# A one-core hybrid transformer layer on Trainium2: normalising products pinned behind the second slot's logits, two gate projections moved forward

## The chip, the cores and the metric

The kernel runs on one core of one Trainium2 chip. The metric is the device time of one execution in microseconds (us). The median of three runs of the kernel before is 888.42 us (888.24 to 889.56).

The engines have short names in what follows: PE multiplies matrices, DVE, ACT and POOL work on vectors, SP issues the DMA transfers. Every engine works through its own queue in order.

## The reference

One layer of a decoder (512 tokens, width 1024, fp32) with three mixers side by side:

```python
h = rms_norm(x, g_mix)
qa, ka, va, xb, gb, qc, kc, vc, gates = split(h @ w_in)
o_a = sum(softmax(lses, axis=0) * outs)       # outs, lses of the 3 groups of mixer A
o_b = rg_lru_branch(xb, gb)
o_c = moba_attention(qc, kc, vc)
gt = sigmoid(gates).reshape(B, S, 3, D)
merged = gt[:, :, 0] * (o_a @ p_a) + gt[:, :, 1] * (o_b @ p_b) + gt[:, :, 2] * (o_c @ p_c)
x = x + merged @ w_out
gate, up = split(rms_norm(x, g_ffn) @ w_gu)
x = x + (silu(gate) * up) @ w_down
return rms_norm(x, g_final)
```

Mixer A is a dilated window attention in 3 groups of 4 heads (dilations 1, 4, 16); slot j of the three groups is combined by their softmax denominators. Mixer B is a convolution and an RG-LRU scan times a GeLU gate, mixer C a block-sparse attention with 8 heads.

## The kernel before

**Products.** Every fp32 number is held as a high and a low part (hi, lo), and every product is three matmuls (`mm3`, lines 200 to 202): hi by hi, lo by hi, hi by lo. A projection (`project`) of 128 output columns is 8 such triples, 24 matmuls of 128x512, into one of the 8 PSUM banks.

**Weights.** `chunk_plan` lists the 512 KB chunks of weights in the order in which PE will want them. Each chunk passes through three engines: SP loads it (wraw, three buffers), ACT casts the high part (whi, L178, four buffers), and POOL, for chunks 7 to 61, subtracts the low part (wlo, L183, four pieces of 128x256); DVE does that for the others.

**x and its normalised form.** X holds the eight pairs (hi, lo) of x times the norm's gain g. The norm's factor per token, rb, is known only later, so projections that use X are multiplied by rb (or rq, for queries) when they leave PSUM (L479). XN holds the pairs of x·g·rb and needs no such step. `reload` fetches x again (8 DMAs) and `renorm` makes XN: for each of 8 tiles one product on DVE (L926, x·g·rb), then `split`: a cast on ACT for hi (L249) and a subtraction on DVE for lo (L250). Projections of half 1 of mixer A, of mixer C, of mixer B and all 24 gates use XN.

**Mixer A in slots.** The heads are worked on in four slots j = 0 to 3, each with its own dictionary d0 to d3. `la(j)` gives the steps for the logits, which are woven between the matmuls of another projection: group 0 with 128x256 logits and their row minima (L562), then the two class groups, whose bias is added at L579 and whose minima (m, stp) are taken at L585. `wa(d)` takes the exponentials on ACT (L594), adds two sums on DVE (L710) and sends the slot's statistics through DRAM (exch) and back in another order. `wa2(d)` works out each group's weight (ee on ACT, the rest on DVE) and scales the probabilities P (L599). `ta(d)` turns P on PE (L608, L622), and ACT and DVE split the result into ph, pl (L611, L612) and pp (L628, L629). `xa(d)` multiplies with the values (L659, L780).

**Gates.** `gate` is one projection and a tanh; the results wait as z tiles until `merge` uses them. Of 24, the table `EARLY` says how many are worked out at which place ahead of merge; merge does the others, staying `G_LEAD` = 2 ahead. The place names are a2, a3, v0 and so on; a new place has to stand in `EARLY`, in `chunk_plan` and in the program.

**What sets the order.** A scheduler reorders each engine's instructions by its own model of their times, within what the data allow; `keep_in_program_order` pins an instruction to its place in the program. The program's own order around the change is: values of A with slot 0's logits woven in, `wa(d0)`, `fa(0, 2, 0)` and `fa(0, 2, 1)` (the q and k projections of the last pair of half 0), `wa2(d0)`, `renorm`, slot 1's logits in the first values of C, `wa(d1)`, `ta(d0)` in the second values of C, `fa(1, 0, 0)`, `xa(d0)`, `fa(1, 0, 1)`.

Of the kernel before, what the change touches and what calls it, by code (L numbers as in the profile page):

```python
# [9 lines left out]
AF = mybir.ActivationFunctionType  # L10
ALU = mybir.AluOpType
# [7 lines left out]
KT = 8  # L19
# [24 lines left out]
N_POOL = 62  # L44
AHEAD = 2

EARLY = {"a2": 1, "a3": 1, "v0": 2, "v1": 2, "v2": 1, "c0": 1, "c1": 1, "l1": 1, "l2": 1, "l3": 1, "l4": 1,
         "b0": 1, "b1": 4}
G_LEAD = 2
N_WARM = 10  # L50
# [5 lines left out]
def chunk_plan():  # L56
# [3 lines left out]
    def a(h, i, w):  # L60
        plan.append(("ma", (OFF_QA, OFF_KA)[w], A_PAIRS[h][i]))

    def v(off, g):
        plan.extend(("v", off + g * 256, kh) for kh in range(2))
# [18 lines left out]
    plan.extend(("vv", OFF_VA + 256, kq) for kq in range(4))  # L83
    a(0, 2, 0)
    a(0, 2, 1)
    v(OFF_VC, 0)
    v(OFF_VC, 1)
    for n in range(2):
        a(1, n, 0)
        a(1, n, 1)  # L90
    a(1, 2, 0)
    g("a2")
    a(1, 2, 1)
# [38 lines left out]
def layer_kernel(tc, x0p, xT, wts, tab, oneh, msk, idn, gfin, out):  # L132
    nc = tc.nc
# [3 lines left out]
    with (  # L137
# [91 lines left out]
        def project(act, kind="m", steps=(), first=0):  # L229
            return weave(project_g(act, kind), 8, steps, first)  # L230
# [39 lines left out]
        X = []  # L270
# [403 lines left out]
                qk[pair[n] + (w,)] = t[n]  # L674

        def fa(half, i, w, steps=(), first=0):
            scaled = half == 1
            ea(project(XN if scaled else X, "ma", steps, first), half, i, w, scaled)

        def st_part(st, s, o):  # L680
# [225 lines left out]
        def gate(steps=()):  # L906
            ng[0] += 1
            z = slot(F32, "z")
            nc.scalar.activation(z, project(XN, "m", steps), AF.Tanh, scale=0.5)
            return z  # L910


        XN = []
# [6 lines left out]
                nc.sync.dma_start(xt, xT[k])  # L920
                x_again.append(xt)

        def renorm(ks):
            for k in ks:
                xt = x_again[k]
                nc.vector.scalar_tensor_tensor(xt, in0=xt, scalar=prm[:, k : k + 1], in1=rb,  # L926
                                               op0=ALU.mult, op1=ALU.mult)
                XN.append(split(xt))

        zs = []  # L930
# [2 lines left out]
        def early(place, steps=()):  # L933

            n = EARLY[place]
            for i in range(n):
                zs.append(gate(steps if i == n - 1 else ()))
# [25 lines left out]
        wa(d0)  # L963
        fa(0, 2, 0)
        fa(0, 2, 1)
        wa2(d0)
        renorm(range(8))
        d1, st = la(1)
        VC.append(values_out(values_mm(st, 12)))
        wa(d1)  # L970
        st = ta(d0)
        VC.append(values_out(values_mm(st)))
        fa(1, 0, 0)
# [2 lines left out]
        wa2(d1)  # L976
        fa(1, 1, 0)
        fa(1, 1, 1)
        st = ta(d1)
        fa(1, 2, 0, st)  # L980
        early("a2")
# [360 lines left out]
```

## Time and profile before

| | us |
|---|---|
| median of 3 runs | 888.42 |
| lowest, highest | 888.24, 889.56 |
| profiled execution | 888.6 |
| its span | 886.6 |
| PE busy in it | 875.2 (99%) |
| DVE, ACT, POOL busy | 472.8, 399.3, 283.9 |

The profile is of one execution. Its span runs from the first to the last instruction; 2.0 us of the 888.6 lie around it. The chain of work that ended last runs through PE for 88% of the span. PE's busy time counts a matmul as busy at whatever clock it was granted, so a slow clock shows in no idle time; the profile gives the granted clock by itself, as a share of 2.4 GHz, and its lower level, 1.2 GHz, reads 0.50.

### The profile page before, as it was taken

To read this page: it belongs to the slowest core of one execution; us is meant where nothing else is said; L and a number is where in the kernel's file an instruction comes from. 1 tells how busy PE (TensorE), PEld (TensorE's weight loads), DVE (VectorE), ACT (ScalarE), POOL (GpSimd) and SP (SyncE) were. 2 spreads that over 40 slices of the span, in tenths; PEclk is the share of its full clock that TensorE was granted. 3 is DMA by queue.
4 is the path that set the end of the run, shared out by engine and by line. 5 is a ranking of instruction groups with operands and counts; after the bars stand their busy time and mean duration, and the time that the engine had idled before them with its cause. 6 is when DMAs were issued, how large, how long until landed. Compare 5 with 4: busy or idle time off the path is not lost.

```text
span 886.6 us, 11269 instructions
## 1 busy us (share of the span) xinstructions
PE 875.2 (99%) x4166; PEld 737.4 (83%) x4166; DVE 472.8 (53%) x922; ACT 399.3 (45%) x692; POOL 283.9 (32%) x328
## 2 busy tenths in 40 slices
PE   9999999999999999999999999999999999999996
PEld 7897988888888888888888888888888888888885
DVE  7498947566665656647425445444444444322226
ACT  7376754664675567762323434333223332222213
POOL 2157364655543434675111312111222111000004
PEclk9999999999999999999999999999999999999999
DMA  7247332652322221232223322222222222222202
GB/s 276 93 158 111 94 127 88 108 133 96 95 95 84 84 95 47 97 119 95 95 95 119 119 92 84 88 94 95 95 95 99 100 103 104 96 95 95 95 24 96
DMA packets 40279, 90.28 MB, mean 102 GB/s; under 512 B 13988, under 2 KB 15780, under 8 KB 40224
## 3 DMA queue, kind: packets, MB, share of 16 engines
q1 hardware_dynamic: 34048, 88.26, 30.8%
q10 hardware_dynamic: 5824, 0.98, 0.7%
q8 instruction: 33, 0.54, 0.3%
q0 software_dynamic: 352, 0.33, 0.2%
q14 instruction: 22, 0.18, 0.1%
HBM read 87.34 MB, written 2.20 MB: 101 GB/s over the span
## 4 chain that ended last, share of the span: by engine, by line
PE 88%; DVE 4%; issue 3%; POOL 2%; DMA 2%; ACT 1%; DVEq 0%; POOLq 0%; ACTq 0%
PE ps L200 23%; PE ps L201 23%; PE ps L202 23%; PE ps L1189 12%; POOL wlo L183 2%; DMA wraw<-in_wts 2%; PE ps L659 2%; PE ps L608 1%; PE ps L555 1%; PE ps L554 1%; DVE y L1234 1%; DVE lo L250 0%; PE ps L622 0%; PE ps L780 0%; ACT junk L1220 0%
## 5 line engine op out<-in xcount | busy, mean ns | idle before, releaser
L178 ACT CAST whi<-wraw 128x1024 fp32r<-128x1024 f32 (+1 forms) x149 | 154.6, 1039 | 274.9 <-issue 101.5
L183 POOL TENSOR_TENSOR wlo<-wraw,whi 128x256 fp32r<-128x256 f32 x220 | 169.6, 803 | 181.1 <-ACT whi L178 181.0
L200 PE MATMUL ps<-hi,whi 128*128 128x512 f32 x520 | 205.2, 395 | 0.0
L201 PE MATMUL ps<-lo,whi 128*128 128x512 f32 x520 | 202.9, 390 | 0.0
L202 PE MATMUL ps<-hi,wlo 128*128 128x512 f32 x520 | 202.7, 390 | 0.0
L183 DVE TENSOR_TENSOR wlo<-wraw,whi 128x1024 fp32r<-128x1024 f32 (+1 forms) x94 | 117.5, 1250 | 115.5 <-ACT whi L178 115.5
L200 PE MATMUL ps<-uhi,whi 128*128 128x512 f32 x352 | 137.9, 392 | 0.0
L202 PE MATMUL ps<-uhi,wlo 128*128 128x512 f32 x352 | 137.1, 389 | 0.0
L201 PE MATMUL ps<-ulo,whi 128*128 128x512 f32 x352 | 136.9, 389 | 0.0
L202 PEld LDWEIGHTS ps<-hi,wlo 128*128 128x128 f32 x520 | 97.6, 188 | 20.6
L200 PEld LDWEIGHTS ps<-hi,whi 128*128 128x128 f32 x520 | 97.7, 188 | 18.8
L201 PEld LDWEIGHTS ps<-lo,whi 128*128 128x128 f32 x520 | 97.8, 188 | 18.5
L1163 POOL TENSOR_TENSOR av<-sg,uu 128x512 f32<-128x512 f32 x22 | 45.7, 2077 | 198.5 <-DVE sg L1161 198.5
L202 PEld LDWEIGHTS ps<-uhi,wlo 128*128 128x128 f32 x352 | 66.1, 188 | 14.0
L201 PEld LDWEIGHTS ps<-ulo,whi 128*128 128x128 f32 x352 | 66.1, 188 | 13.5
L200 PEld LDWEIGHTS ps<-uhi,whi 128*128 128x128 f32 x352 | 66.1, 188 | 13.3
L1189 PE MATMUL ps<-wlo,hi 128*128 128x512 f32 (+1 forms) x180 | 57.7, 384 | 0.0
L1189 PE MATMUL ps<-whi,lo 128*128 128x512 f32 (+1 forms) x180 | 57.7, 384 | 0.0
L1189 PE MATMUL ps<-whi,hi 128*128 128x512 f32 (+1 forms) x180 | 57.1, 384 | 0.0
L1159 DVE TENSOR_TENSOR uu<-ps,rb 128x512 f32<-128x512 f32 x22 | 15.2, 690 | 64.9 <-PE ps L202 64.9
L1222 POOL TENSOR_TENSOR y<-x,gf 128x512 f32<-128x512 f32 (+1 forms) x8 | 9.7, 1229 | 108.3 <-DVE x L1212 107.9
L200 PE MATMUL ps<-whi,xhi 128*128 128x256 f32 (+1 forms) x128 | 40.4, 318 | 0.3 <-DVE stn L562 0.3
(232 smaller groups left out, 1236.2 us busy)
## 6 DMA issues: line engine op xcount, KB each, us to landing
wraw<-in_wts SPq DMA_DIRECT2D x145, 512.0 KB, 3.2
xt<-in_xT SPq DMA_DIRECT2D x15, 256.0 KB, 5.5
bias<-relb SPq DMA_DIRECT2D x8, 256.0 KB, 6.9
xr<-in_xT SPq DMA_DIRECT2D x8, 256.0 KB, 2.7
out<-y SPq DMA_DIRECT2D x7, 256.0 KB, 2.4
wraw<-in_wts SPq DMA_DIRECT2D x4, 256.0 KB, 4.9
bias<-relb SPq DMA_DIRECT2D x4, 128.0 KB, 4.5
bias<-relb SPq DMA_DIRECT2D x8, 64.0 KB, 5.1
```

The source lines that it names most:

```text
L178: nc.scalar.copy(hi[:, cc], raw[:, cc])
L183: eng.tensor_sub(lo[:, dd], raw[:, dd], f32(hi[:, dd]))
L200: nc.tensor.matmul(o, lh, rh, start=start, stop=False)
L201: nc.tensor.matmul(o, lh, rl, start=False, stop=False)
L202: nc.tensor.matmul(o, ll, rh, start=False, stop=stop)
L554: nc.tensor.matmul(bk, qh[:, qc], kk[:, k0 : k0 + nn], start=True, stop=False)
L555: nc.tensor.matmul(bk, ql[:, qc], kk[:, k0 : k0 + nn], start=False, stop=True)
L659: nc.tensor.matmul(po[:, o0 : o0 + n], vf(kt), p, start=(i == 0), stop=(i == len(mms) - 1))
L1159: nc.vector.tensor_mul(uu, pu, r2)
L1163: nc.gpsimd.tensor_mul(av, sg, uu)
L1189: nc.tensor.matmul((acc[tb][hf] if o is None else o)[:, cc], l[:, t], r[:, hf * 512 + cc.start : hf * 512 + cc.stop], start=((k == 0 or fi ...
L1222: eng.tensor_mul(y2[hf][:, cc], x, gf[hf][:, cc])
```

## The change

Four things change. `EARLY` gains the places a0 and a1, one gate each. a0 stands behind `fa(0, 2, 1)`, ahead of slot 1's logits; a1 behind `fa(1, 1, 1)`, ahead of `ta(d1)`. Merge then has two gates fewer to do. `renorm` moves from ahead of `la(1)` to behind `wa(d1)`; all eight products come first, each pinned in program order, and the eight splits follow. Since XN does not exist yet at a0 and at `fa(1, 0, *)`, these use X: the gate gets a multiplication by rb on DVE ahead of its tanh, and q and k of `fa(1, 0, *)` the multiplication that half 0 has. In the changed kernel the lines of the code shown below are two to ten further down: 926 becomes 933, 562 becomes 564, 612 becomes 614.

```diff
-EARLY = {"a2": 1, "a3": 1, "v0": 2, "v1": 2, "v2": 1, "c0": 1, "c1": 1, "l1": 1, "l2": 1, "l3": 1, "l4": 1,
+EARLY = {"a0": 1, "a1": 1, "a2": 1, "a3": 1, "v0": 2, "v1": 2, "v2": 1, "c0": 1, "c1": 1, "l1": 1, "l2": 1, "l3": 1, "l4": 1,
         "b0": 1, "b1": 4}
...
     a(0, 2, 0)
     a(0, 2, 1)
+    g("a0")
     v(OFF_VC, 0)
     v(OFF_VC, 1)
     for n in range(2):
         a(1, n, 0)
         a(1, n, 1)
+    g("a1")
     a(1, 2, 0)
...
         def fa(half, i, w, steps=(), first=0):
-            scaled = half == 1
+            scaled = (half, i) > (1, 0)
...
             z = slot(F32, "z")
-            nc.scalar.activation(z, project(XN, "m", steps), AF.Tanh, scale=0.5)
+            if XN:
+                nc.scalar.activation(z, project(XN, "m", steps), AF.Tanh, scale=0.5)
+            else:
+                nc.vector.tensor_mul(z, project(X, "m", steps), rb)
+                nc.scalar.activation(z, z, AF.Tanh, scale=0.5)
...
-        def renorm(ks):
-            for k in ks:
+        def renorm():
+            for k in range(KT):
                 xt = x_again[k]
-                nc.vector.scalar_tensor_tensor(xt, in0=xt, scalar=prm[:, k : k + 1], in1=rb,
-                                               op0=ALU.mult, op1=ALU.mult)
+
+                tc.keep_in_program_order(nc.vector.scalar_tensor_tensor(
+                    xt, in0=xt, scalar=prm[:, k : k + 1], in1=rb, op0=ALU.mult, op1=ALU.mult))
+            for xt in x_again:
                 XN.append(split(xt))
...
         fa(0, 2, 0)
         fa(0, 2, 1)
+        early("a0")
         wa2(d0)
-        renorm(range(8))
         d1, st = la(1)
         VC.append(values_out(values_mm(st, 12)))
         wa(d1)
+        renorm()
         st = ta(d0)
...
         fa(1, 1, 1)
+        early("a1")
         st = ta(d1)
```

**DVE, slot 0's logits.** The queue of before, from the end of the values' evictions (v) to the first class minimum (m):

```order
L455 SCALAR_TENSOR_TENSOR v_567<-ps_482,mixr_361,v_567 128x4x64
L926 SCALAR_TENSOR_TENSOR xt_117_570<-xt_117_570,prm,rb_410 128x512
...
L926 SCALAR_TENSOR_TENSOR xt_119_574<-xt_119_574,prm,rb_410 128x512
L562 ISA P_673,stn_586<-ps_675,bias_671 128x128
...
L926 SCALAR_TENSOR_TENSOR xt_120_576<-xt_120_576,prm,rb_410 128x512
L926 SCALAR_TENSOR_TENSOR xt_121_578<-xt_121_578,prm,rb_410 128x512
L579 TENSOR_TENSOR P_706<-ps_707,bias_704 128x256
L579 TENSOR_TENSOR P_706<-ps_713,bias_704 128x256
L926 SCALAR_TENSOR_TENSOR xt_122_580<-xt_122_580,prm,rb_410 128x512
...
L926 SCALAR_TENSOR_TENSOR xt_124_584<-xt_124_584,prm,rb_410 128x512
L585 ISA P_706,m_127_588<-ps_707,P_706 128x128
```

And after the change:

```order
L457 SCALAR_TENSOR_TENSOR v_567<-ps_482,mixr_361,v_567 128x4x64
L564 ISA P_673,stn_586<-ps_675,bias_671 128x128
...
L581 TENSOR_TENSOR P_706<-ps_707,bias_704 128x256
L581 TENSOR_TENSOR P_706<-ps_713,bias_704 128x256
L587 ISA P_706,m_127_588<-ps_707,P_706 128x128
```

The eight products are gone from there, so the logits follow one another.

**DVE, from slot 1's last logits to the first turned weights of slot 0 (pl).** Before:

```order
L585 ISA P_1130,stp_992<-ps_1137,P_1130,m_214_993 128x128
...
L599 TENSOR_SCALAR P_706<-P_706,ff_941 128x128 x4
L599 TENSOR_SCALAR P_745<-P_745,ff_941 128x128 x4
L710 TENSOR_TENSOR stp_992<-dd_1174 128x4
L455 SCALAR_TENSOR_TENSOR v_1167<-ps_1061,mixr_361,v_1167 128x4x64
L612 TENSOR_TENSOR pl_1234<-ps_1228,ph_1233 128x512
```

After:

```order
L587 ISA P_1127,stp_989<-ps_1134,P_1127,m_203_990 128x128
...
L457 SCALAR_TENSOR_TENSOR v_1161<-ps_1058,mixr_361,v_1161 128x4x64
L712 TENSOR_TENSOR stp_989<-dd_1171 128x4
L933 SCALAR_TENSOR_TENSOR xt_117_570<-xt_117_570,prm,rb_410 128x512
...
L933 SCALAR_TENSOR_TENSOR xt_124_584<-xt_124_584,prm,rb_410 128x512
L252 TENSOR_TENSOR lo_1194<-xt_117_570,hi_1193 128x512
...
L252 TENSOR_TENSOR lo_1222<-xt_124_584,hi_1221 128x512
L614 TENSOR_TENSOR pl_1271<-ps_1265,ph_1270 128x512
```

Eight products and eight low parts now stand between the sum of slot 1's exponentials (L712) and pl; the scaling of slot 0's P (L599) has moved ahead of slot 1's logits, and the low parts no longer lie there.

**PE, from `fa(0, 2, 1)` (ps_869) to the first values of C.** Before:

```order
L202 MATMUL ps_869<-xhi_152,wlo_727 128x512
L200 MATMUL ps_1012<-whi_816,xhi_104 128x256
L201 MATMUL ps_1012<-wlo_817,xhi_104 128x256
...
L202 MATMUL ps_1012<-whi_861,xlo_154 128x256
L554 MATMUL ps_1069<-kk_896,qh_851 128x256
```

After:

```order
L204 MATMUL ps_869<-xhi_152,wlo_727 128x512
L202 MATMUL ps_919<-xhi_104,whi_816 128x512
...
L204 MATMUL ps_919<-xhi_152,wlo_817 128x512
L202 MATMUL ps_1009<-whi_861,xhi_104 128x256
...
L204 MATMUL ps_1009<-whi_911,xlo_154 128x256
```

The 24 matmuls of gate a0 (ps_919) stand between the k projection and the values, ahead of slot 1's logits, and take the chunk that the values took before.

## Rows read from the trace of the kernel before

**Rows 1.** The page's busy times: engine, us, share of the span, instructions.

```profile
PE 875.2 (99%) x4166; PEld 737.4 (83%) x4166; DVE 472.8 (53%) x922; ACT 399.3 (45%) x692; POOL 283.9 (32%) x328
```

**Rows 2.** Stretches: length, busy PE, PEld, DVE, ACT, POOL; PE's clock, DMA share, GB/s.

```profile
72.00:74.00 2.00, 0.37 (x2) 0.35 (x3) 2.00 (x10) 0.00 (x0) 2.00 (x3) 1.00 0.67 33
76.00:78.00 2.00, 2.00 (x6) 1.52 (x6) 1.27 (x5) 2.00 (x10) 0.00 (x0) 0.50 0.47 25
```

**Rows 3.** PE in order of time: start, duration, instruction, idle time before and its releaser.

```profile
71.03 0.40 PE L202 MATMUL ps<-whi,xlo 128*128 128x512 f32 x1
73.63 0.47 PE L200 MATMUL ps<-xhi,whi 128*128 128x512 f32 x1 [2.20 <-DVE m L585]
...
74.87 0.63 PE L202 MATMUL ps<-xhi,wlo 128*128 128x512 f32 x1
...
78.28 0.39 PE L201 MATMUL ps<-xlo,whi 128*128 128x512 f32 x1
...
80.34 0.39 PE L201 MATMUL ps<-xlo,whi 128*128 128x512 f32 x1
```

**Rows 4.** DVE in order of time, the same columns, around slot 0's logits.

```profile
63.27 3.14 DVE L926 SCALAR_TENSOR_TENSOR xt<-xt,prm,rb 128x512 f32<-128x512 f32 x3 [0.32 <-DMA xt<-in_xT]
...
70.05 3.01 DVE L926 SCALAR_TENSOR_TENSOR xt<-xt,prm,rb 128x512 f32<-128x512 f32 x3
```

**Rows 5.** Groups by line, 62 to 75 us: busy us, mean ns, idle before.

```profile
L183 POOL TENSOR_TENSOR wlo<-wraw,whi 128x256 fp32r<-128x256 f32 x12 | 12.0, 1030 | 8.4 <-ACT whi L178 8.4
L926 DVE SCALAR_TENSOR_TENSOR xt<-xt,prm,rb 128x512 f32<-128x512 f32 x8 | 8.0, 1054 | 0.3 <-DMA xt<-in_xT 0.3
```

**Rows 6.** POOL in order of time: the low parts of weights.

```profile
62.14 7.93 POOL L183 TENSOR_TENSOR wlo<-wraw,whi 128x256 fp32r<-128x256 f32 x8 [8.14 <-ACT whi L178]
70.30 4.05 POOL L183 TENSOR_TENSOR wlo<-wraw,whi 128x256 fp32r<-128x256 f32 x4 [0.23 <-ACT whi L178]
```

**Rows 7.** PE in order of time, 99 to 109 us.

```profile
99.55 0.28 PE L202 MATMUL ps<-whi,xlo 128*128 128x256 f32 x1
100.14 0.36 PE L200 MATMUL ps<-whi,xhi 128*128 128x256 f32 x1 [0.32 <-DVE stn L562]
...
102.73 0.60 PE L608 MATMUL ps<-ident,P 128*128 128x128 f32 x4
...
108.16 0.87 PE L622 MATMUL ps<-ident,P 128*128 128x128 f32 x4
```

**Rows 8.** Groups by line, 92 to 112 us.

```profile
L183 POOL TENSOR_TENSOR wlo<-wraw,whi 128x256 fp32r<-128x256 f32 x8 | 5.6, 747 | 11.3 <-ACT whi L178 11.3
L250 DVE TENSOR_TENSOR lo<-xt,hi 128x512 fp32r<-128x512 f32 x8 | 5.3, 680 | 0.0
L249 ACT CAST hi<-xt 128x512 fp32r<-128x512 f32 x7 | 3.8, 614 | 0.0
...
L594 ACT ACTIVATE P<-P,stp 128x128 f32<-128x128 f32 x8 | 3.1, 400 | 0.0
L178 ACT CAST whi<-wraw 128x1024 fp32r<-128x1024 f32 x2 | 2.1, 1037 | 0.0
...
L733 ACT ACTIVATE ee<-df 128x8 f32<-128x8 f32 x2 | 0.4, 204 | 1.0 <-DVE df L731 1.0
```

**Rows 9.** One stretch of merge, columns as in the second group.

```profile
400.00:420.00 20.00, 20.00 (x90) 16.58 (x89) 14.06 (x17) 6.00 (x7) 11.71 (x7) 1.00 0.33 106
```

**Rows 10.** A group by line of the whole span: multiplications that empty a PSUM bank.

```profile
L479 DVE TENSOR_TENSOR kt<-ps,rb 128x512 f32<-128x512 f32 x3 | 2.1, 692 | 0.1
```

**Rows 11.** DVE in order of time, from kk's end to pl.

```profile
89.97 2.98 DVE L519 TENSOR_TENSOR kk<-kt,kk 64x256 fp32r<-64x256 f32 x4 [0.26 <-ACT kk L517]
...
109.78 1.19 DVE L612 TENSOR_TENSOR pl<-ps,ph 128x512 fp32r<-128x512 f32 x2
```

**Rows 12.** The chain that ended last, in order of time: start, us, what.

```profile
70.09 11.59 DMA wraw<-in_wts
...
119.23 0.95 PE ps L659 x8
```

## The prediction

> **What bounds the kernel now.** I read the page's line of busy times first: PE is busy 99% of the span [rows 1], so the kernel can only become faster where PE stands still or runs slowly, and a step moved between DVE, ACT and PE's queue matters only through that. The table by stretches then shows the one place where both happen. In 72 to 74 us PE is busy for 0.37 of 2 us, DVE and POOL for all of it; in 76 to 78 us PE is busy throughout, at a granted clock of 0.50, the lower of its two levels [rows 2]. PE's list in order of time gives the cause: the first matmul of slot 0's q projection starts at 73.63 after 2.20 us idle, released by DVE's class maximum (m, L585); from 74.87 to 78.28 eight matmuls then come 0.43 us apart, where nine later ones, 78.28 to 80.34, come 0.23 apart [rows 3]. The full bank of slot 0's logits is what PE waits for, and DVE empties it late because the eight products of renorm lie between the logits: three at 63.27, two in the middle, three more at 70.05 [rows 4], 8.0 us in all, next to POOL's weight subtractions all the while [rows 5].
>
> **What the change takes away.** Behind the change the eight products are no longer ahead of or among slot 0's logits. (1) The stall: 73.63−71.03 = 2.60, less one normal spacing of 0.23, is 2.37 [rows 3]. PE would ask for the bank 71.26; with 8.0 us of products gone from in front of it [rows 5] DVE has freed it by 73.6−8.0 = 65.6, or a little later if the logits themselves arrive later, so a margin of some 5 us. PE's next input, the weight chunk of that projection, ends its low part at 62.14+7.93 = 70.07 [rows 6], 1.2 before it is wanted, and earlier if POOL runs alone. (2) The slow clock: 3.41−8×0.23 = 1.58 [rows 3]. In this trace the clock falls behind the standstill and nowhere nearby; I take it that without a standstill it does not fall. (3) Slot 1's logits: PE waits 100.14−99.55 = 0.59, less 0.12 for a matmul of 256 columns, 0.47, for a bank freed by stn (L562) [rows 7]; DVE was late there through the eight low parts of x (L250, 5.3 us [rows 8]), which leave that place too, while a0 gives DVE 5.5 us more. (4) The turning of the class weights waits a little for its scaled P: four transposes take 0.87 at 108.16 where four others take 0.60 [rows 7], so 0.27; in the new order P is scaled before slot 1's logits, far ahead. Sum: 2.37+1.58+0.47+0.27 = 4.69 us.
>
> **What it adds and moves.** Two gate projections are moved, not added: 24 matmuls of 0.23, 5.5 us each, at either place. At the old place, in merge, PE is busy all 20 us of a sampled stretch with DVE at 14.06 [rows 9]; nothing there waits for the gates to cover it, so I cost the removal at nothing. If it did need them, DVE's 6 us of slack in 20 would be the first to go, at most some tenths. a0's own weight chunk has its low part at 70.30+4.05 = 74.35 [rows 6] and PE wants it at about 82, so it does not wait. a0 works on the unnormalised x: one extra DVE multiplication from PSUM, like kt's, 0.69 [rows 10], and fa(1,0,*) two more, behind everything that PE waits for. All 210 issues of SP's queue remain; the weight loads only carry other chunks. The z tiles live longer, in a pool of 70; PE's order gives no sign of a wait for one, and I cost that at nothing.
>
> The cost is in DVE's queue ahead of ta(d0). The first half of slot 0's turned weights (pl, L612) is now behind eight products and eight low parts. Before: from the end of kk at 89.97+2.98 = 92.95 to the end of the pl pair at 109.78+1.19 = 110.97 are 18.0 us [rows 11], the eight low parts among them. PE first uses them at 119.23 [rows 12], so 8.3 us of slack. After, DVE has in the same stretch, besides: a0's multiplication, 0.69; a wait ahead of L710's sum for slot 1's exponentials, which before was filled by scaling P: eight exponentials, 3.1, and a weight cast, 1.04, on ACT [rows 8], of which some 0.8 runs beside the last logits, so 3.3; two round trips to ACT for ee, which the low parts filled before: 0.21 of work each [rows 8], by estimate 0.5 with the way, 1.0; and the products. No row has these products with POOL idle. Their lower bound is 5.3, from the eight low parts of the same size (0.68 each) with POOL idle for most of the stretch [rows 8]; the upper is their own 8.0 next to POOL [rows 5]. So 18.0+0.7+3.3+1.0+5.3 = 28.3 up to 31.0. The start, kk's end, moves with q's cast on ACT, which stands behind the cast of a chunk whose load took 11.59 us from 70.09 [rows 12]; that load can start up to 2 us sooner if POOL is not slowed, so kk ends between 90.95 and 92.95. The pair ends at 119.3 to 124.0, its first tile 0.5 earlier, 118.8 to 123.5. PE is there at 119.23+5.5 (a0)−4.7 (gained) = 120.0. So the wait is between none (1.2 us spare) and 3.5 us. I take none: with slot 1 behind it POOL has 11.3 us idle in 20 [rows 8], and the row nearest to that is 0.68. ACT's eight hi casts move along, 0.61 each [rows 8]: each runs beside the next product, and what queues behind them is ph, ready two casts after the last product while DVE still has low parts to do, and the weight chunks of fa(1,1,*), which PE wants behind fa(1,0,*), 11 us later. Then ACT once more: the last cast of the second class pair (pp) now queues behind a weight cast that waits for the end of fa(1,0,0), which is where PE turns to the products; 1.04 for that cast [rows 8] and about 0.8 for the pp pieces, against some 1.5 us of matmuls that come first (0.95 of them L659 [rows 12]): between 0 and 0.4, I take 0.3.
>
> **A rule of the Trainium skill.** In one stretch DVE's products take 1.05 us and POOL's subtractions 1.03 [rows 5]; in the other DVE's subtractions of the same tile size take 0.68 and POOL's 0.75 [rows 8]: where POOL never rests, both engines are slower. The skill's page "SBUF — State Buffer", section "Who interferes with whom", has a rule that speaks against this change: a DVE instruction with both inputs in SBUF contends with a GpSimd instruction that reads SBUF, and whichever issues second stands still for the whole of the other. The trace agrees with it in the two pairs of numbers. By that rule each of the sixteen instructions that meets a POOL piece from its start would take up to 0.75 longer, 12.0 us in all, where the rows as I take them give nothing; rival B stands on the measured 1.05 instead.
>
> **The rivals.** A: *the pl chain arrives a little late.* The products cost near their old 1.05 [rows 5], or the load is not earlier; PE stands some 2 of the possible 3.5 us at xa(d0), and the clock drops once more for 1.58 [rows 3]: 884.0+2.0+1.6 = 887.6. For it: 1.2 us to spare is little beside a chain of 28; against it: POOL's idle time [rows 8]. Chance 0.14. B, **slower**: *DVE and POOL hold each other up at the new place.* POOL's chunks fall on all sixteen instructions, each takes the measured 1.05 [rows 5], and the load is not earlier: 16×1.05 = 16.8 in place of the 10.6 that I take, 6.2 longer; with the start 2.0 later and 1.2 to spare the wait is 7.0, and 1.6 of slow clock: 884.0+8.6 = 892.6. It ends slower from a wait of 4.6 on (884.0+4.6+1.6 = 890.2). Against it: in 20 us POOL has two chunks, 5.6 us, and sixteen instructions of DVE need 10.6 [rows 8], so about half of them can meet one. Chance 0.07. C: *the change does not do what it says.* The bank is free, but another input is late at 71.26 (the weights have 1.2 us to spare [rows 6]), PE stands still anyway and the clock falls behind it: 884.0+2.4+1.6 = 888.0, down to 886.5 where the standstill is shorter. Against it: POOL's work there was slowed by the products themselves. Chance 0.06. The rest, 0.05, is what I don't see, either way.
>
> **How the numbers follow.** −4.69+0.3 = −4.4; on the profiled execution, 888.6 (span 886.6 and 2.0 around it), that is 884.2. The median of the three runs is 888.42, 0.2 below it, so the forecast is 884.0. Its own band is 883.3 (nothing at pp, and some tenths of an estimate too low) to 885.3 (the two smaller terms not gained and a little more at pp), chance 0.68. A measurement of this kernel tells about 0.2%, 1.8 us, from no change: faster is below 886.6, slower above 890.2. Faster: 0.68, a third of A (0.05), a sixth of C (0.01) and 0.02 of the rest, 0.76. Same: what is left of A and C (0.14) and 0.02 of the rest, 0.16. Slower: B and 0.01 of the rest, 0.08. The range from 883.1 to 888.0 takes in the forecast, most of A and C, and leaves out B, the end of A and the rest.
>
> **What would show it.** Right: between 70 and 80 us no PE idle time above 0.3 and a granted clock of 1.0; no wait for stn near 100; the products (now L933) as a block near 108 to 115 at 0.7 us each; the first L661 of slot 0 with less than 0.5 us idle. A: the same, with 1 to 3.5 us idle at L661 released by pl, and a clock of 0.5 behind it. B: there, products above 1 us and POOL busy beside them. C: idle time at 71 released by something other than m. The forecast is wrong if PE's idle time at xa(d0) exceeds 1 us, or if the clock falls without a standstill.

## The result and the profile after

The changed kernel is slower. Its median is 895.25 us (894.88 to 898.46, 6 runs) beside 889.51 (888.24 to 889.82, 6 runs) for the kernel before: a ratio of 1.0075, with a 95% interval of 1.0063 to 1.0086. The forecast was 884.0, the range 883.1 to 888.0.

The profiled execution took 898.46 us, the longest of the six, with a span of 896.4, 9.8 longer than that of before. The page's busy times answer to [rows 1]:

```profile
PE 880.6 (98%) x4166; PEld 741.1 (83%) x4166; DVE 476.4 (53%) x925; ACT 402.0 (45%) x692; POOL 282.6 (32%) x328
```

The two stretches of [rows 2], with the same columns (length; busy PE, PEld, DVE, ACT, POOL; clock; DMA share; GB/s), show that what the forecast took from this place was there to be had:

```profile
72.00:74.00 2.00, 2.00 (x11) 1.70 (x10) 0.74 (x3) 2.00 (x10) 0.56 (x1) 1.00 1.79 31
76.00:78.00 2.00, 2.00 (x10) 1.66 (x9) 0.38 (x1) 0.00 (x0) 2.00 (x4) 1.00 1.30 26
```

PE is busy for all of both, at the full clock. But the list of what PE waits for (total us, times, longest) has entries further on that the kernel before did not have:

```profile
PE ps L202 <- DVE stn L564: 3.1, 1, 3.1
PE ps L624 <- DVE P L601: 2.2, 4, 1.0
PE ps L661 <- POOL ph L616: 1.1, 1, 1.1
...
PE ps L661 <- DVE pl L614: 0.4, 1, 0.4
```

These are three places: slot 1's logits (stn), the values of slot 0 (pl, ph) and the turning of slot 1's class weights (P). PE in order of time gives where they are:

```profile
105.56 0.55 PE L202 MATMUL ps<-whi,xhi 128*128 128x256 f32 x1 [3.08 <-DVE stn L564]
...
126.14 0.39 PE L661 MATMUL ps<-pl,v 128*128 128x256 f32 x1 [0.38 <-DVE pl L614]
...
128.34 0.39 PE L661 MATMUL ps<-ph,v 128*128 128x256 f32 x1 [1.12 <-POOL ph L616]
...
159.43 0.33 PE L624 MATMUL ps<-ident,P 128*128 128x128 f32 x1 [1.04 <-DVE P L601]
```

Behind each of the three the clock falls. The stretches, columns as above; the first lies in a part of the program that the change does not touch, and 14 of the 16 kernels profiled here have it (0.68 to 0.88), the one before not:

```profile
30.00:35.00 5.00, 5.00 (x29) 5.00 (x30) 2.12 (x12) 1.01 (x2) 2.29 (x4) 0.83 0.32 104
...
106.00:112.00 6.00, 6.00 (x44) 6.00 (x44) 4.62 (x25) 5.50 (x18) 2.85 (x4) 0.80 0.35 55
120.00:130.00 10.00, 8.49 (x39) 6.71 (x38) 8.50 (x17) 6.91 (x13) 7.65 (x9) 0.94 0.44 133
130.00:140.00 10.00, 10.00 (x44) 8.23 (x43) 7.75 (x11) 6.02 (x10) 6.51 (x9) 0.88 0.39 139
160.00:170.00 10.00, 8.66 (x32) 6.59 (x33) 7.75 (x17) 4.92 (x11) 5.17 (x9) 0.83 0.16 54
```

From the distances between PE's matmuls, less what the same matmuls take at full clock, the 9.8 us of the two profiled executions divide so:

| place in the trace of after | us against before |
|---|---|
| 30 to 41 us, clock 0.83 at first, before 1.00 | +1.3 |
| slot 0's logits: stall and slow clock gone | −4.2 |
| slot 1's logits: stall 3.24 where before had 0.47 | +2.8 |
| thirteen matmuls at half clock behind it | +1.3 |
| values of slot 0 (L661): waits 1.8, slow clock 1.6 | +3.4 |
| turning slot 1's weights (L624): waits 3.6, slow clock 1.6 | +5.2 |

They sum to 9.8; single rows are sure to about half a us. The first row is no cost of the change, which leaves 8.5 for it in these two executions; the medians are 5.7 apart, so the profiled execution of after is a costly one.

What made slot 1's logits late is seen on ACT, in order of time (an ACTq row is an issue to a DMA queue):

```profile
68.07 0.42 ACTq L720 DMA_DIRECT2D exch<-stn  x1
...
75.40 0.47 ACT L456 ACTIVATE v<-ps,mixr 128x256 fp32r<-128x256 f32 x1
84.61 0.45 ACTq L720 DMA_DIRECT2D exch<-stp  x1
85.11 1.21 ACT L456 ACTIVATE v<-ps,mixr 128x256 fp32r<-128x256 f32 x3 [9.24 <-DMA exch<-stn]
```

ACT reaches the second write of slot 0's statistics (stp) at 75.9 and is idle for 9.2 us there, the issue included, until the first write (stn), issued at 68.07, has landed. Before, ACT came later, after the first write had landed (68.65 and 9.6 us to landing, 78.3), and did not stop:

```profile
79.37 0.38 ACTq L718 DMA_DIRECT2D exch<-stp  x1
```

```profile
exch<-stn ACTq DMA_DIRECT2D x1, 4.0 KB, 9.6
```

Transfers are late here in themselves as well. The weight load that SP issued at 69.16 took 16.4 us and landed at 85.56, so ACT could not have cast that chunk, which stands ahead of q's cast, much before it did, at 86.19. And SP stood 13.0 us at the read-back of the first write, with the next weight load behind it in its queue. DVE pays for ACT's stop: it has nothing to do until ACT's part of v is there, and everything behind is late.

```profile
85.62 1.27 DVE L457 SCALAR_TENSOR_TENSOR v<-ps,mixr,v 128x256 fp32r<-128x256 f32 x3 [9.23 <-ACT v L456]
...
94.69 2.71 DVE L521 TENSOR_TENSOR kk<-kt,kk 64x256 fp32r<-64x256 f32 x4 [0.20 <-ACT kk L519]
...
114.34 4.62 DVE L933 SCALAR_TENSOR_TENSOR xt<-xt,prm,rb 128x512 f32<-128x512 f32 x6
...
119.27 1.40 DVE L933 SCALAR_TENSOR_TENSOR xt<-xt,prm,rb 128x512 f32<-128x512 f32 x2
120.59 4.89 DVE L252 TENSOR_TENSOR lo<-xt,hi 128x512 fp32r<-128x512 f32 x8
125.41 1.14 DVE L614 TENSOR_TENSOR pl<-ps,ph 128x512 fp32r<-128x512 f32 x2
```

kk ends at 97.40 where it ended at 92.95 before [rows 11], and the pl pair at 126.55.

### The profile page after: what moved, and what is told of

Its sections match the earlier page's. It is cut to its first block, busy times and chain, and to the rows that moved or that the text cites. A ratio compares the mean times of both kernels' runs of the same rounds, so it can differ in the third digit from the quotient of the medians.

```text
span 896.4 us, 11289 instructions
## 1 busy us (share of the span) xinstructions
PE 880.6 (98%) x4166; PEld 741.1 (83%) x4166; DVE 476.4 (53%) x925; ACT 402.0 (45%) x692; POOL 282.6 (32%) x328
## 4 chain that ended last, share of the span: by engine, by line
PE 87%; DVE 7%; ACT 2%; DMA 2%; issue 1%; POOL 0%; ACTq 0%; DVEq 0%; POOLq 0%
PE ps L202 23%; PE ps L203 23%; PE ps L204 23%; PE ps L1199 12%; DMA exch<-stn 2%; DVE kk L521 2%; PE ps L661 2%; PE ps L610 1%; DVE P L601 1%; PE ps L557 1%; PE ps L556 1%; DVE qq L471 1%; DVE y L1244 1%; PE ps L782 0%; ACT junk L1230 0%
## 5 line engine op out<-in xcount | busy, mean ns | idle before, releaser
L202 PE MATMUL ps<-hi,whi 128*128 128x512 f32 x496 | 196.8, 397 | 0.0
L203 PE MATMUL ps<-lo,whi 128*128 128x512 f32 x496 | 194.1, 391 | 0.0
L204 PE MATMUL ps<-hi,wlo 128*128 128x512 f32 x496 | 194.0, 391 | 0.0
L204 PEld LDWEIGHTS ps<-hi,wlo 128*128 128x128 f32 x496 | 93.6, 189 | 20.0
L203 PEld LDWEIGHTS ps<-lo,whi 128*128 128x128 f32 x496 | 93.8, 189 | 18.0
L202 PEld LDWEIGHTS ps<-hi,whi 128*128 128x128 f32 x496 | 93.6, 189 | 17.8
L204 PEld LDWEIGHTS ps<-uhi,wlo 128*128 128x128 f32 x352 | 66.1, 188 | 13.8
```

Of the source, the lines that this page charges most:

```text
L202: nc.tensor.matmul(o, lh, rh, start=start, stop=False)
L203: nc.tensor.matmul(o, lh, rl, start=False, stop=False)
L204: nc.tensor.matmul(o, ll, rh, start=False, stop=stop)
```

## The experiments

The theory from the trace was that ACT's stop at the second write costs most of the time, through a wait for the buffer that both writes share. Its rivals: the wait is for a completion semaphore; the transfers are slow in themselves and would stop ACT elsewhere; and a large part comes from the chain behind pl, whatever ACT does at 76 us. Each kernel was timed beside the kernel before on the same chip, and a ratio is against that one. Where two kernels below ran on different chips, the difference of their medians and that of their ratios can lie up to 1.3 us apart. Edits are to the changed kernel unless the text says otherwise.

**Two buffers for the two writes.** Is it the shared DRAM tile that makes the second write wait?

```diff
-        exch = dr.tile([4, 4 * 512], F32)
+        exch = [dr.tile([4, 2 * 512], F32, name=f"exch{n}") for n in range(2)]
...
-                return bass.AP(tensor=a.tensor, offset=a.offset + n * 1024, ap=ap)
+                a = exch[n][j : j + 1, :]
+                return bass.AP(tensor=a.tensor, offset=a.offset, ap=ap)
```

> The changed kernel with one thing different: each of a slot's two writes of its statistics goes to a DRAM buffer of its own (before: two parts of one buffer), so the second write on ACT's queue need not wait until the first has landed; order of all engines unchanged. Theory 1 (ACT's queue stood 9.2 us at the second write, and the q casts, the k casts and slot 1's logits behind it were late): ACT idle before the second write under 1 us, q's cast 3 to 4 us sooner (then held by the weight chunk that lands near 82), no PE wait at slot 1's logits (3.1 in the changed kernel), pl 3 to 4 us sooner and no wait at L661, 885 to 888 us. Theory 2 (the chain of products and low parts ahead of pl is too long by itself): the 3.1 us wait goes, but PE still waits over 1 us at L661 and at L624, with the slow clock behind them: 890 to 892 us.

Measured: 896.32 us (896.01 to 897.99), ratio 1.0079 (1.0064 to 1.0094). ACT still stops at the second write, and still for the first:

```profile
82.62 1.20 ACT L456 ACTIVATE v<-ps,mixr 128x256 fp32r<-128x256 f32 x3 [6.54 <-DMA exch<-stn]
```

So it is not the buffer. The compiled kernel's instructions show another link: each transfer that SP or ACT issues signals its end through one of eight completion semaphores, taken in turn, and an issue waits until the last transfer that used its semaphore has ended. In the changed kernel the two writes of slot 0 are one turn apart and share a semaphore; before, the second write shared one with a bias load that had long landed.

**The same edit to the kernel before.**

> The kernel before with the same two buffers. Theory 1: no change (within 0.2%), since there the first write has landed at 78.26 when ACT comes to the second at 79.37. Theory 2: no change either. A gain of over 1 us would mean that the wait cost the kernel before as well.

Measured: 891.36 us (888.15 to 892.56), ratio 1.0015 (1.0004 to 1.0027), a little slower where no change was expected. Its profile has a wait of 1.6 for stn, where before has 0.3, and 1.2 for P, which before does not have; why is open. The stall at slot 0's logits is there as before, but the eight matmuls at half clock behind it are not. So the slow clock does not follow this standstill every time.

**The gates alone**, renorm where it was before:

```diff
-            scaled = (half, i) > (1, 0)
+            scaled = half == 1
...
         wa2(d0)
+        renorm(range(8))
         d1, st = la(1)
...
         wa(d1)
-        renorm()
```

> The kernel before with the two gates moved forward and nothing else (renorm stays ahead of slot 1's logits and its products are not pinned). Both theories: the 2.2 us wait at slot 0's logits and the slow clock behind it stay; the second write of the statistics comes late (near 79) and does not stop ACT; slot 1's logits have 5.5 us more and no wait for stn: 887.5 to 889 us. If the gates themselves hurt (a missing cover in merge, a late chunk), over 890.

Measured: 887.62 us (886.05 to 889.53), ratio 0.9976 (0.9966 to 0.9985): faster. What PE waits for:

```profile
PE ps L202 <- DVE m L587: 2.2, 1, 2.2
```

Of the entries named above only this stall of before is left, with no slow clock behind it; the one for stn is gone. So a gate of 5.5 us ahead of slot 1's logits gives DVE the time that it lacked there, and merge did not need its two gates.

**Renorm alone**, without the two gates:

```diff
-EARLY = {"a0": 1, "a1": 1, "a2": 1, "a3": 1,
+EARLY = {"a2": 1, "a3": 1,
...
-        early("a0")
...
-        early("a1")
```

> The changed kernel without the two gates: renorm behind slot 1's logits, products pinned, q and k of fa(1,0) from X. Theory 1: no wait at slot 0's logits, ACT stops 8 to 10 us at the second write as in the changed kernel, and since a0's 5.5 us of PE work are missing ahead of slot 1's logits PE waits there 6 to 9 us: 897 to 901 us. Theory 2 (only the chain ahead of pl counts): PE waits at L661 about 5 us longer than in the changed kernel, little at slot 1's logits.

Measured: 899.67 us (898.7 to 901.74), ratio 1.0116 (1.0101 to 1.0131).

```profile
PE ps L622 <- DVE P L599: 4.0, 2, 3.5
PE ps L554 <- DVE kk L524: 2.6, 1, 2.6
PE ps L608 <- DVE P L599: 1.1, 3, 0.5
```

The whole loss is in moving renorm, with the detour of q and k through X that it brings. Without a0's cover PE comes to slot 1's logits before kk is there, and the turning of P costs more.

**Another turn of the semaphores.** A copy of 16 bytes shifts the turn by one; the order on DVE, ACT and POOL stays.

```diff
+        spare = dr.tile([1, 4], F32, name="spare")
...
+            if j == 0:
+                nc.sync.dma_start(spare, stp[0:1, 0:4])
```

> The changed kernel with one 16-byte transfer more (a spare copy of four statistics to an unused DRAM buffer, SP's queue, after slot 0's statistics). In the program the transfers take completion semaphores in turn and each waits for the last user of its own; in the changed kernel the two writes of slot 0's statistics are exactly one turn apart and so have the same one, with the spare transfer they are not. Order on DVE, ACT and POOL unchanged. Theory 1' (ACT stood for the first write's end through that shared semaphore, and everything behind it was late): ACT issues the second write near 76 to 77 with under 1 us idle, the next weight cast waits for its chunk until about 82, q's cast starts near 83 (87.5 in the changed kernel), slot 1's logits cost PE no wait (3.1), pl 4 us sooner, no wait at L661: 884 to 888 us. Theory 2 (the products and low parts ahead of pl are too long by themselves): ACT's stop goes, but waits of over 1 us at L661 and at L624 with the slow clock behind them stay: 890 to 893 us.

Measured: 893.68 us (893.24 to 895.4), ratio 1.0055 (1.0042 to 1.0069). ACT's stop, then what PE waits for:

```profile
80.20 1.21 ACT L456 ACTIVATE v<-ps,mixr 128x256 fp32r<-128x256 f32 x3 [5.59 <-DMA bias<-relb]
```

```profile
PE ps L624 <- DVE P L601: 2.4, 5, 1.0
PE ps L661 <- DVE pl L614: 1.7, 1, 1.7
PE ps L661 <- POOL ph L616: 1.1, 1, 1.1
```

The second write now waits for whatever used its new semaphore last, a bias load, 5.6 us in place of 9.2. That a transfer of other data takes over the wait shows the semaphore as its cause. kk ends at 92.89, slot 1's logits no longer wait, and the time falls by 1.6. The larger part of the loss is still there: pl is late by 1.7 although kk is as early as before, and P is late.

**Splits behind the values of C.** Only the products stay ahead of pl; once with the spare copy and once without.

```diff
                     xt, in0=xt, scalar=prm[:, k : k + 1], in1=rb, op0=ALU.mult, op1=ALU.mult))
+
+        def resplit():
             for xt in x_again:
                 XN.append(split(xt))
...
         VC.append(values_out(values_mm(st)))
+        resplit()
         fa(1, 0, 0)
```

> As the run with the spare transfer, and the eight splits of the normalised x moved behind the values of C, so that only the eight products stand ahead of pl on DVE. Theory 1': within 1 us of the run with the spare transfer alone, since pl was in time there. Theory 2: 3 us or more faster than it, with pl 5 us sooner.

> The changed kernel with only the splits moved behind the values of C; ACT still stops at the second write. Theory 1': the 3.1 us wait at slot 1's logits stays, the waits at L661 go: 892 to 894 us. Theory 2: most of the loss goes, 886 to 888 us.

Measured, with the copy: 890.99 us (889.84 to 893.48), ratio 1.0022 (1.0012 to 1.0031); without: 893.49 us (891.52 to 893.9), ratio 1.0041 (1.0027 to 1.0054). With the copy the entries are

```profile
PE ps L610 <- DVE P L601: 2.8, 2, 2.4
...
PE ps L624 <- DVE P L601: 0.8, 2, 0.4
```

The wait at L661 is gone in both, and the loss from P stays. Four kernels then stand side by side: 895.25, 893.68 (copy), 893.49 (late splits), 890.99 (both). The copy gives 1.6 and the splits 1.8 alone, together 4.3 (by the ratios 1.8, 3.0 and 4.7).

**k of fa(1, 0, 1) from the normalised x.** In the changed kernel it uses X, since XN is not there when q is worked out. With the spare copy:

```diff
-            scaled = (half, i) > (1, 0)
+            scaled = (half, i, w) > (1, 0, 0)
```

> The kernel with the spare transfer, and the k projection of fa(1,0) (not its q) from the normalised x. Its k tiles then come straight from PSUM, and their cast on ACT stands ahead of the weight cast that waits for PE, not behind it (in the run with the spare transfer alone DVE is idle 4.8 us for that cast, and slot 1's scaled P, k tiles and transposes come late behind it). Theory 3 (a second wait at the head of ACT's queue makes ta(d1) late): waits at L624 and the slow clock near 155 us go, the waits at L661 stay, 2.5 to 4 us less than the run with the spare transfer alone: 890 to 891 us. Theory 2 (DVE has too much work in 105 to 160 us, wherever ACT stands): the waits at L624 stay at over 1 us, within 1 us of that run.

Measured: 889.61 us (887.38 to 891.1), ratio 1.0001 (0.9992 to 1.001): 4.1 less than with the copy alone (by the ratios 4.8). The wait at L624 is gone, the others are not:

```profile
PE ps L661 <- DVE pl L614: 1.6, 1, 1.6
PE ps L661 <- POOL ph L616: 1.1, 1, 1.1
```

The way from k to P is seen on ACT in the changed kernel:

```profile
142.18 1.05 ACT L180 CAST whi<-wraw 128x1024 fp32r<-128x1024 f32 x1 [3.91 <-PE ps L203]
143.13 0.62 ACT L525 CAST kk<-kt 64x512 fp32r<-64x512 f32 x1
```

k is taken from PSUM into kt by DVE first, at 137.30; its casts on ACT then stand behind a weight cast that waits 3.9 us for PE to give a buffer back. DVE waits 4.8 us for the first of them, and all of wa2(d1), its P last, comes behind kk. With XN, ACT takes k from PSUM in its turn, ahead of that cast, as before.

**Products behind slot 0's sum.** If the products are hard to place behind slot 1, they might go behind slot 0, with the gates kept; the splits stand behind wa2(d0).

```diff
-            scaled = (half, i) > (1, 0)
+            scaled = half == 1
...
-            nc.vector.tensor_add(st_part(stp, 1, 0), dd[:, 0:4], dd[:, 4:8])
+            tot = nc.vector.tensor_add(st_part(stp, 1, 0), dd[:, 0:4], dd[:, 4:8])
+            if j == 0:
+                tc.keep_in_program_order(tot)
...
         wa(d0)
+        renorm()
         fa(0, 2, 0)
...
         wa2(d0)
+        resplit()
...
         wa(d1)
-        renorm()
```

> The kernel with the two gates moved, and the eight products pinned behind the sum of slot 0's exponentials (where DVE is idle in the changed kernel, 76 to 86 us) in place of behind slot 1's; the splits where they were before. Theory 4 (what matters is DVE's free time: pin them where DVE waits for something else): no wait at slot 0's logits, none over 0.3 us at slot 1's, at L661 and at L624; the gain of the prediction without its price: 883 to 885.5 us. If ACT's stop for the first write of the statistics matters by itself (the second write shares its completion semaphore here too), a wait of 1 to 3 us at slot 1's logits and 886 to 889 us.

Measured: 891.17 us (888.57 to 893.01), ratio 1.002 (1.0009 to 1.0031); the gain did not come. ACT:

```profile
83.23 1.05 ACT L180 CAST whi<-wraw 128x1024 fp32r<-128x1024 f32 x1 [6.16 <-DMA wraw<-in_wts]
...
88.27 1.05 ACT L180 CAST whi<-wraw 128x1024 fp32r<-128x1024 f32 x1 [3.98 <-DMA wraw<-in_wts]
89.22 1.28 ACT L500 ACTIVATE qh<-qt 64x512 fp32r<-64x512 f32 x2
```

The products are where they should be, 77.77 to 83.71 at 0.74 each, and PE does not stop at slot 0. But q's cast comes at 89.22, behind weight casts that wait 6.2 and 4.0 us for their loads, so kk is late again (98.41) and PE waits 3.9 for stn. The first of the two loads was issued at 69.26 and took 13.9 us; the second was issued only at 83.07, since SP stood 9.4 us at the read-back of the first write.

**The same with the spare copy.**

> As the run with the products pinned behind slot 0's sum, with the spare transfer, so that the second write does not share its semaphore with the first. Theory 4: within 0.5 us of the run without the spare transfer. If ACT's stop matters there, 1 us or more faster than it.

Measured: 890.01 us (889.02 to 892.29), ratio 1.0013 (1.0002 to 1.0024). ACT's weight casts stand 5.9 us for a load and 3.3 us for what the profile names as the second write; the load that this cast needs landed at 87.03 (issued at 82.03, 5.0 us), just ahead of the cast at 87.08, so it is rather that. PE waits 3.4 for stn. The median is 1.2 us lower, but the two intervals overlap: a gain from another turn of the semaphores is not shown here, and ACT is late as before.

**The second write from SP**, so that no wait for a semaphore stops ACT:

```diff
-                nc.scalar.dma_start(dram(n, n), st[:, 0:8])
+                (nc.scalar, nc.sync)[n].dma_start(dram(n, n), st[:, 0:8])
```

> The changed kernel with the second write of each slot's statistics issued from SP's queue in place of ACT's; ACT's order is otherwise the same. Theory 1'' (ACT's stop at that write is the whole of the loss ahead of slot 1's logits): ACT works on at 76 us, q's cast starts at 77 to 79, no wait at slot 1's logits, kk ends 5 us sooner than in the run with the spare transfer (92.9), the waits at L661 go: 888 to 890 us. Theory 5 (ACT stops a few instructions later anyway, at a weight cast whose chunk lands late, since the transfers themselves are slow): q's cast starts at 82 or later, kk ends at 92 to 93, 892 to 894 us as in the run with the spare transfer.

Measured: 893.41 us (893.15 to 894.47), ratio 1.005 (1.0035 to 1.0065). ACT:

```profile
82.06 1.05 ACT L180 CAST whi<-wraw 128x1024 fp32r<-128x1024 f32 x1 [5.21 <-DMA wraw<-in_wts]
83.02 1.28 ACT L500 ACTIVATE qh<-qt 64x512 fp32r<-64x512 f32 x2
```

It passes the write and stops a few instructions further, at a weight cast whose load is late; kk ends at 92.79, as with the spare copy. So two things hold ACT there: the semaphore, and behind it a load that is slow while the first write is under way. This load, issued at 69.06, landed at 81.96, 1.1 us after the write had; in the changed kernel it landed 1.0 us after it. ACT's stop at the write is therefore worth little beyond the load's own lateness, 1.6 to 1.8 us by this run and the one with the copy.

**The first write in pieces of 16 bytes.** It consists of 1024 pieces of 4 bytes; laid out like the second it has 256. Slot 0's first statistics then come back in a wrong order, so its softmax weights are wrong; the work is the same.

```diff
-                nc.scalar.dma_start(dram(n, n), st[:, 0:8])
+                nc.scalar.dma_start(dram(n, 1 if j == 0 else n), st[:, 0:8])
```

> The changed kernel with slot 0's first write of statistics in pieces of 16 bytes in place of 4 (a quarter of the pieces); the statistics arrive in another order, so the softmax weights of slot 0 are wrong, everything else is the same. Theory 5: the write lands within 4 us (16.5 in the changed kernel), the weight chunk behind it lands 5 us or more sooner, ACT does not stop over 2 us, kk ends at 88 to 90, no waits at slot 1's logits or L661: 888 to 890 us. If the 4-byte pieces are not what slows the transfers, the write still takes over 9 us and the time is 894 to 896.

Measured: 891.19 us (889.55 to 891.9), ratio 1.0019 (1.001 to 1.0028), 4.1 below the changed kernel. The issues between 66 and 86 us (KB each, median us to landing), in the changed kernel and here:

```profile
exch<-stn ACTq DMA_DIRECT2D x1, 4.0 KB, 16.5
```

```profile
exch<-stn ACTq DMA_DIRECT2D x1, 4.0 KB, 7.7
```

And the weight load that SP issues at 69.16, in the changed kernel and here:

```profile
wraw<-in_wts SPq DMA_DIRECT2D x1, 512.0 KB, 16.4
```

```profile
wraw<-in_wts SPq DMA_DIRECT2D x1, 512.0 KB, 9.7
```

The write did not land within the 4 us that were expected, but it takes less than half of its time, and the load lands 6.7 us sooner with it. The second write goes out at 75.88 with 0.5 us of waiting, q's cast comes at 79.95, kk ends at 89.78, and the waits for stn and at L661 are gone. What is left is P, 2.6 at L624 and 0.7 at L610, as it must be if that has a cause of its own. No run has both this write and k from XN, so how near the two together come to the forecast is not shown.

**The same edit to the kernel before.**

> The kernel before with the same 16-byte write (softmax weights of slot 0 wrong). Theory 5: the chunk of 11.6 us lands in about 4, but PE does not wait for it there; the stall at slot 0's logits stays: within 1 us of the kernel before.

Measured: 889.54 us (888.06 to 889.78), ratio 1.0000 (0.9991 to 1.001). The write lands in 4.2 us in place of 9.6 and the load next to it in 4.9 in place of 11.6. Before, nobody waited for them, so quick ones gain nothing.

**Products behind slot 0, with ACT freed**: the kernel with the products behind slot 0's sum, the second write on SP, and q's casts pinned ahead of the casts of chunks 14 and 15.

```diff
-                nc.scalar.copy(hi[:, cc], raw[:, cc])
+                cast = nc.scalar.copy(hi[:, cc], raw[:, cc])
+                if i in (14, 15):
+                    tc.keep_in_program_order(cast)
...
+            pin = tc.keep_in_program_order if pos[0] == 13 else (lambda x: x)
...
-                    nc.scalar.activation(qh[halves(d), :], tmp[c, :], AF.Copy, scale=s_)
+                    pin(nc.scalar.activation(qh[halves(d), :], tmp[c, :], AF.Copy, scale=s_))
...
-                nc.scalar.dma_start(dram(n, n), st[:, 0:8])
+                (nc.scalar, nc.sync)[n].dma_start(dram(n, n), st[:, 0:8])
```

> The run with the products pinned behind slot 0's sum, the second write on SP's queue, and q's casts pinned on ACT ahead of the next two weight casts, so that nothing that waits for a transfer stands ahead of q and k on ACT. If the position of the products is right and only ACT's queue spoiled it: no wait over 0.5 us at slot 0's and slot 1's logits, 884 to 887 us. If DVE's work is what counts: a wait of 2 to 4 us at slot 1's logits as in that run, 889 to 891 us.

Measured: 886.79 us (884.54 to 888.66), ratio 0.9973 (0.9964 to 0.9983), with the gates alone the fastest of all; the two intervals overlap, so neither beats the other. The time is the one that the first theory expected, but the wait of 2.1 us that is left on PE is the second's. The profiled execution, 888.66, is the longest of the ten.

```profile
PE ps L204 <- DVE stn L567: 2.1, 1, 2.1
```

q and kk are not what is late: kk ends at 93.10 here, and with the gates alone it ended at 94.41 without a wait for stn. PE, which no longer stands at slot 0, comes sooner, and DVE is slower between kk and the first of stn (10.9 us against 8.5). Its four scalings of slot 0's P, and POOL beside them:

```profile
98.66 3.01 DVE L604 TENSOR_SCALAR P<-P,ff 128x128 f32<-128x128 f32 x4
```

```profile
98.13 7.17 POOL L187 TENSOR_TENSOR wlo<-wraw,whi 128x256 fp32r<-128x256 f32 x8 [2.63 <-ACT whi L180]
```

With the gates alone POOL has nothing to do at that time, and the same four take

```profile
98.73 1.07 DVE L601 TENSOR_SCALAR P<-P,ff 128x128 f32<-128x128 f32 x4
```

So the stall has moved from slot 0 to slot 1. That POOL's work beside DVE makes it is likely; no run takes POOL away there.

## Why the prediction was wrong

**The gains were right.** Term (1), 2.37, and term (2), 1.58, come to 3.95; the trace shows 4.0 to 4.2. That a0 gives DVE its time at slot 1, and that the gates cost nothing, is what the kernel with the gates alone shows. Term (4) came too: from 108.4 to 125.4 us no two matmuls start more than 0.3 apart, the four transposes among them, and the 0.3 set down for pp was not paid. Rival C is out: no other input was late at slot 0. The time went past rival B's 892.6, but by other mechanisms than that one's. 1.1 us of the miss is the base: the forecast started from 888.42, the median of three runs of the kernel before, and six give 889.51.

**The step that failed first: "so kk ends between 90.95 and 92.95".** It followed q's cast on ACT back to a weight load and asked only whether that load would start sooner. The load did, by 0.9 us (69.16 against 70.09), but it took 16.4 us in place of the 11.59 that the step carried over, and landed at 85.56, where the range needs 79.7 to 81.7. Nor did the step ask what else ACT's queue now meets sooner. The second write is an issue in that queue, the change brings it forward from 79.37 to 75.9, and ACT stood there until the first write had landed, 16.5 us after its issue. Both ends of the range rested on the load keeping its time and on the write going out at once, as it had before, when it came late enough for that. kk ended at 97.40, outside the range by 4.45, and so (3) turned from a gain of 0.47 into a stall of 3.24. The slow pair of transfers weighs more than ACT's stop: a quicker first write, which ends the stop and quickens the load too, gave 4.1 us; the write on SP, which ends the stop alone, gave 1.8, and the copy, which shortens it, 1.6. The list of DMA issues of before had a sign of it, that write at 9.6 us and the load next to it at 11.6, where the page's median for such a load is 3.2. The size was not to be had there: by 9.6 us ACT would have stopped for some 2 us (68.07+9.6−75.9), and which semaphore the second write would share stands in no trace of before. What is to be learnt is that an instruction that waits for nothing in a trace may only have come late.

**The chain from kk to pl was sized rightly, and its lower end taken wrongly.** Predicted were 28.3 to 31.0; measured are 126.55−97.40 = 29.15, and 29.16 with the spare copy. That kernel is the forecast's case with kk at 92.89: PE comes to xa(d0) at 119.7, predicted 120.0, and the pl pair ends at 122.05, within the predicted 119.3 to 124.0. The text took no wait, from a spare of 1.2 us against an uncertainty of 4.7. The middle of its own range, 121.65, was the better choice and is rival A. DVE's products and low parts did cost about what was forecast, 6.0 and 4.9 us (before 5.3 for the low parts, [rows 8]).

**POOL stood in no step.** The wait of 1.1 at L661 is for a clearing of ph on POOL, which is queued behind a weight chunk of four pieces. This is the chunk's first piece, and the clearing:

```profile
122.35 3.73 POOL L185 TENSOR_TENSOR wlo<-wraw,whi 128x256 fp32r<-128x256 f32 x1 [7.26 <-ACT whi L180]
128.09 0.20 POOL L616 MEMSET ph<- 128x128 f32 x1
```

The piece starts among DVE's low parts and ends 0.6 us after the last of them (125.48); the other three take 0.73 each, and the whole chunk 5.79, where the one at 112.26 took 2.83, for the most part ahead of the products. All seven kernels profiled here that have the eight low parts in one block ahead of pl show one such piece, of 3.71 to 3.73 us, and no other does. Rival B had the two engines hold each other up with DVE as the payer, 16 instructions at 1.05. Here the eight low parts take 4.89 in all, as without a neighbour, and POOL takes 3.0 longer. The Trainium skill's page "SBUF — State Buffer", section "Who interferes with whom", has the engine that issues second stand still for the whole of the other's instruction; the trace agrees that one of the two stands still, but POOL's piece stood through five instructions of DVE in a row, not one, and the forecast had weighed the rule for DVE only.

**A step was missing: fa(1, 0, 1).** The text costs the two extra multiplications there "behind everything that PE waits for" and stops. The multiplication also changes how k leaves PSUM: through DVE first, so that its casts fall behind a weight cast on ACT that waits for PE. From there the delay runs through kk and P into the turning of slot 1's weights, 2.2 us of waits by PE's list and 5.2 us in the matmuls' distances. Taking it away gave 4.1 us, as much as the quicker write.

**The slow clock.** The forecast tied its 1.58 to a standstill. All three new standstills have it behind them, at 1.3 to 1.6 each. But the kernels with two buffers before and with the gates alone stall 2.6 us at slot 0 and show none behind it; of the four profiles with that stall two have it. And the stretch at 30 to 35 us has 0.83 with no standstill ahead of it. So a standstill has no fixed price in clock: here it was nothing or 1.3 to 1.6 us.

**What stays open.** Why the first write takes 12.7 to 16.5 us in the changed kernel and its variants and 9.6 before, with the same 1024 pieces, no run settles. That the size of its pieces is part of it is shown, 7.7 us with 256 of them; that its neighbours in the queues are the rest is only likely: it is issued 1.7 us after the weight load ahead of it in the changed kernel (66.37 and 68.07), 2.8 before (65.88 and 68.65). Why the profiled execution lies 3.2 above the median is open too. The 1.3 at 30 us do not explain it, since nearly every profile has them; its first write, at 16.5 us, is the slowest of all, and the two kernels that keep ACT's stop and the gates, with two buffers and with late splits, have 13.8 and 15.1 us and waits for stn of 1.6 and 1.9 in place of 3.1.

## What to carry to other kernels

When a step is freed, walk every queue that it speeds up to the next DMA issue and ask what that issue waits for; one that went out at once before may have done so only because it came late. Do not carry a transfer's time over when what is issued around it moves. When a change alters the route by which a value leaves PSUM, follow that value to its last reader. Where the spare time is smaller than the width of the range it comes from, forecast from the middle of the range, and try the halves of a change apart: here one half alone was faster by 0.24% and the other slower by 1.2%.

## What was not expected of the hardware

A transfer that one engine issues can be held back by a transfer of other data: in this compiled kernel eight completion semaphores go round, and the engine that issues stands still until the last user of its semaphore is done, 9.2 us for the first write, 5.6 for a bias load after a shift of one. And a write of 4 KB in pieces of 4 bytes is slow, 16.5 us to landing where 16-byte pieces took 7.7 in the same place, and a 512 KB load next to it is slow with it, 16.4 us against 9.7; with the write on SP such a load stopped ACT 5.2 us by itself. One POOL subtraction stood 3.73 us beside a block of DVE's, where its neighbours took 0.73, and DVE lost nothing by it.
